# A token mixer without GpSimd: wide head norms, inverse roots by Newton steps on DVE, a sink column, and two projections left in float32

## The chip, the core and the metric

One core of a Trainium2 chip runs the whole program: matrix products on PE (TensorE), elementwise work on DVE (VectorE), ACT (ScalarE) and POOL (GpSimd), loads issued from SP's queue. The metric is the device time of one execution in microseconds. Three executions of the kernel before gave 1207.95, 1210.28 and 1211.51 us; the median, 1210.28 us, is the time before.

## The reference

Two layers of an encoder over 256 tokens of width 1024. A layer is a half-step SwiGLU feed-forward block (FFN, inner width 2816), a token mixer, a second FFN and a gated input embedding. The mixer is what the change is about:

```python
u = rms_norm(h, norm_mix[i])
q, k, v, c, g = jnp.split(u @ w_in[i], splits, axis=-1)      # 512, 128, 128, 1024, 2048 columns
q = rms_norm(q.reshape(B, S, 8, 64), q_norm[i])              # a norm for each head
k = rms_norm(k.reshape(B, S, 2, 64), k_norm[i])
y_attn = window_attention(q, k, v, sink[i], rel_bias) @ w_attn_out[i]
c = c_val * jax.nn.sigmoid(c_gate)                           # c_val, c_gate: halves of c
c = depthwise_conv(c, conv_w[i], conv_b[i])                  # 31 taps, 512 channels
c = jax.nn.silu(layer_norm(c, conv_ln_g[i], conv_ln_b[i]))
y_conv = c @ w_conv_out[i]
g_attn, g_conv = jnp.split(jax.nn.sigmoid(g), 2, axis=-1)
h = h + (g_attn * y_attn + g_conv * y_conv) @ w_o[i]
```

The attention's softmax has one more logit, the sink, which takes weight and gives no value. All inputs are float32.

## The kernel before

Tokens stand in two tiles of 128; a weight is streamed once. `Weights` holds a list of units (loads of up to 1 MB into one of 4 `raw` buffers) and of specs (pieces of 128x1024). `prep_upto` splits each piece into a high part `w_hi` (ACT, L88) and the remainder `w_lo` (DVE, L89), both float32r, into one of 7 pairs of buffers; `get` hands out the next one and prepares the one 6 ahead. `mm3` (L285) makes each product of 128x128 activations with 128x512 weights as three float32r matmuls: high by high (L289), high by low (L290), low by high (L291). Activations are split the same way (`split`, L324). `chunk` runs the products of one output into an accumulator `acc_tile`, of which there are three, and calls the work that empties the accumulator before it (`pending`).

The order on each engine is fixed when the program is built: the framework's scheduler sorts the instructions by priority and by an estimate of when they are ready, and the queues then run in that order. `with_urgency` raises the priority of what it wraps; the taps of the depthwise convolution have the low priority `background`; `ws.later(n, fn)` puts `fn` in front of the n-th weight piece that follows.

The mixer (`mix`, L538) goes through its accumulators in this order: `conv_in(0)` (value and gate of channels 0 to 255), `queries`, `conv_in(2)`, `keys_values`, four `gates`, two `attn_out`, two conv outs (`ps_co`), two outputs of `w_o` (`ps_up`). Beside that run:

- the convolution: after `turn_c` (L584) has put a channel group into `cpad`, 31 taps for each of four channel blocks; blocks 1 to 3 on DVE (first tap L562, the rest L566), block 0 on POOL with two instructions a tap (L559, L560);
- the head norms (`head_norms`, L609): 64-column squares on ACT (L617), `Sqrt` on ACT (L626), reciprocal on DVE, a Newton step of four instructions on POOL (`newton`, L351); then 16 (or 4) scaled copies on ACT (L642, L677), transposes to `qT` and `kT` (L653, L686);
- `scores` (L702): products (L706), bias and row maximum (L716, DVE), negation on POOL, exponentials (L724, ACT), the sink's part on POOL and ACT (L730 to L732), reciprocal, scaling (L735); `attend` transposes the weights (L743), `gather` multiplies by the values (L753);
- the layer norm by token and by channel (L809, L826), whose end (L833) feeds the conv outs, and the splits of `o` (L760) and `y` (L837).

The mean-square norm of the stream (`Norm.finish`, L386) also uses ACT's `Sqrt`, DVE's reciprocal and POOL's Newton step.

## Time and profile before

| what | us |
|---|---|
| executions | 1207.95, 1210.28, 1211.51 (median 1210.28) |
| the profiled execution's own time | 1208.0 |
| its span, first to last instruction | 1206.2 |
| PE busy in the span | 1157.4 (96%) |
| DVE, ACT, POOL busy | 742.5, 625.3, 179.4 |
| mean granted TensorE clock | 0.977 of full speed |

A busy PE is not a PE at its pace: matmuls overlap, and in some stretches the granted clock is half (0.50, which is 1.2 GHz against 2.4 GHz). So the mixer is read by stretches: the time between two starts of the same instruction, the waits of PE with what ended them, and the granted clock. Each time in this text counts from the span's start; the mixer of layer 0 lies between 200 and 380 us, that of layer 1 between 795 and 975 us.

### The profile page before, as it was taken

To read this page: it belongs to the slowest core of one execution; us is meant where nothing else is said; L and a number is where in the kernel's file an instruction comes from. 1 tells how busy PE (TensorE), PEld (TensorE's weight loads), DVE (VectorE), ACT (ScalarE), POOL (GpSimd) and SP (SyncE) were. 2 spreads that over 40 slices of the span, in tenths; PEclk is the share of its full clock that TensorE was granted. 3 is DMA by queue.
4 is the path that set the end of the run, shared out by engine and by line. 5 is a ranking of instruction groups with operands and counts; after the bars stand their busy time and mean duration, and the time that the engine had idled before them with its cause. 6 is when DMAs were issued, how large, how long until landed. Compare 5 with 4: busy or idle time off the path is not lost.

```text
span 1206.2 us, 13732 instructions
## 1 busy us (share of the span) xinstructions
PE 1157.4 (96%) x5138; PEld 923.2 (77%) x5138; DVE 742.5 (62%) x952; ACT 625.3 (52%) x965; POOL 179.4 (15%) x239
## 2 busy tenths in 40 slices
PE   8999999979989999999999999999799899999998
PEld 6778888856667888888878888888566688888886
DVE  6555554689756555545665555557996665555544
ACT  7444444645665545444665444446557555444433
POOL 1000000399300000000100000015990010000001
PEclk9999999978999999999999999999789899999999
DMA  8865455633336565455557555655233365654540
GB/s 280 281 209 198 160 189 180 204 106 74 135 105 183 180 191 188 158 191 174 174 175 209 175 184 183 192 175 177 67 105 121 124 183 184 195 180 158 191 140 36
DMA packets 155360, 202.49 MB, mean 168 GB/s; under 512 B 5284, under 2 KB 108788, under 8 KB 155293
## 3 DMA queue, kind: packets, MB, share of 16 engines
q1 hardware_dynamic: 154204, 200.57, 52.5%
q10 hardware_dynamic: 1088, 1.05, 0.3%
q8 instruction: 40, 0.66, 0.2%
q14 instruction: 28, 0.22, 0.1%
HBM read 200.53 MB, written 1.06 MB: 167 GB/s over the span
## 4 chain that ended last, share of the span: by engine, by line
PE 82%; DVE 6%; POOL 5%; ACT 4%; DMA 2%; issue 1%; SPq 0%; DVEq 0%; ACTq 0%
PE ps_gu L291 13%; PE ps_gu L290 12%; PE ps_gu L289 12%; PE ps_up L291 8%; PE ps_up L289 8%; PE ps_up L290 8%; DVE y L566 3%; POOL part L559 2%; DMA raw<-in_w_ffn_in_dram 2%; PE ps_h L497 2%; PE ps_g L289 1%; PE ps_g L290 1%; POOL y L560 1%; PE ps_g L291 1%; PE ps_o L753 1%
## 5 line engine op out<-in xcount | busy, mean ns | idle before, releaser
L89 DVE TENSOR_TENSOR w_lo<-raw,w_hi 128x1024 fp32r<-128x1024 f32 x376 | 461.4, 1230 | 371.8 <-ACT w_hi L88 371.0
L88 ACT CAST w_hi<-raw 128x1024 fp32r<-128x1024 f32 x376 | 393.6, 1050 | 409.6 <-PE ps_gu L291 192.9
L290 PE MATMUL ps_up<-w_lo,hh 128*128 128x512 f32 x352 | 139.4, 396 | 0.0
L291 PE MATMUL ps_up<-w_hi,hl 128*128 128x512 f32 x352 | 139.4, 396 | 0.0
L289 PE MATMUL ps_up<-w_hi,hh 128*128 128x512 f32 x352 | 139.3, 396 | 0.0
L566 DVE SCALAR_TENSOR_TENSOR y<-cpad,cw,y 128x256 f32<-128x256 f32 x180 | 106.4, 632 | 1.0
L388 POOL TENSOR_TENSOR ms_x<-ss 128x2 f32<-128x2 f32 x8 | 1.7, 217 | 580.8 <-ACT sqj L376 580.8
L291 PEld LDWEIGHTS ps_up<-w_hi,hl 128*128 128x128 f32 x352 | 66.0, 188 | 16.1
L290 PEld LDWEIGHTS ps_up<-w_lo,hh 128*128 128x128 f32 x352 | 66.0, 188 | 15.8
L289 PEld LDWEIGHTS ps_up<-w_hi,hh 128*128 128x128 f32 x352 | 66.0, 188 | 15.7
L559 POOL TENSOR_SCALAR part<-cpad,cw 128x256 f32<-128x256 f32 x60 | 73.3, 1228 | 0.0
L291 PE MATMUL ps_gu<-w_hi,xn0l 128*128 128x512 f32 x176 | 69.1, 395 | 1.2 <-DVE xn0l L327 1.2
L290 PE MATMUL ps_gu<-w_lo,x0h 128*128 128x512 f32 x176 | 70.2, 399 | 0.0
L291 PE MATMUL ps_gu<-w_hi,x0l 128*128 128x512 f32 x176 | 69.7, 396 | 0.0
L290 PE MATMUL ps_gu<-w_lo,xn0h 128*128 128x512 f32 x176 | 69.4, 395 | 0.0
L289 PE MATMUL ps_gu<-w_hi,x0h 128*128 128x512 f32 x176 | 69.4, 394 | 0.0
L290 PE MATMUL ps_gu<-w_lo,xf1h 128*128 128x512 f32 x176 | 69.3, 395 | 0.0
L290 PE MATMUL ps_gu<-w_lo,xf0h 128*128 128x512 f32 x176 | 69.3, 395 | 0.0
L289 PE MATMUL ps_gu<-w_hi,xn0h 128*128 128x512 f32 x176 | 69.0, 393 | 0.0
L291 PE MATMUL ps_gu<-w_hi,xf0l 128*128 128x512 f32 x176 | 69.0, 395 | 0.0
L291 PE MATMUL ps_gu<-w_hi,xf1l 128*128 128x512 f32 x176 | 69.0, 395 | 0.0
L289 PE MATMUL ps_gu<-w_hi,xf1h 128*128 128x512 f32 x176 | 68.9, 393 | 0.0
(234 smaller groups left out, 2078.9 us busy)
## 6 DMA issues: line engine op xcount, KB each, us to landing
raw<-in_w_ffn_in_dram SPq DMA_DIRECT2D x172, 512.0 KB
raw<-in_w_ffn_out_dram SPq DMA_DIRECT2D x40, 1024.0 KB
raw<-in_w_in_dram SPq DMA_DIRECT2D x22, 1024.0 KB
raw<-in_w_in_dram SPq DMA_DIRECT2D x16, 512.0 KB
raw<-in_w_o_dram SPq DMA_DIRECT2D x8, 1024.0 KB
raw<-in_w_pe_gate_dram SPq DMA_DIRECT2D x8, 1024.0 KB
raw<-in_w_ffn_out_dram SPq DMA_DIRECT2D x8, 512.0 KB
raw<-in_w_attn_out_dram SPq DMA_DIRECT2D x8, 512.0 KB
```

The source lines that it names most:

```text
L88: nc.scalar.copy(out=hv[:, :, d0 : d0 + w], in_=src),
L89: nc.vector.tensor_tensor(out=lv[:, :, d0 : d0 + w], in0=src, in1=hv[:, :, d0 : d0 + w].bitcast(F32), op=ALU.subtract,),
L289: nc.tensor.matmul(ps, xh, wh[:, k, :], start=first, stop=False)
L290: nc.tensor.matmul(ps, xh, wl[:, k, :], start=False, stop=False)
L291: nc.tensor.matmul(ps, xl, wh[:, k, :], start=False, stop=last)
L388: nc.gpsimd.tensor_tensor(out=m, in0=self.ss[:, :, 0], in1=self.ss[:, :, 1], op=ALU.add)
L497: nc.tensor.transpose(ps[:, f, tok(t)], hh[:, t, f * P : (f + 1) * P], ident)
L559: nc.gpsimd.tensor_scalar(out=part, in0=src, scalar1=w, scalar2=None, op0=ALU.mult)
L560: nc.gpsimd.tensor_tensor(out=y[:, i, :], in0=part, in1=y[:, i, :], op=ALU.add)
L566: nc.vector.scalar_tensor_tensor(out=y[:, i, :], in0=src, scalar=w, in1=y[:, i, :], op0=ALU.mult, op1=ALU.add)
L753: nc.tensor.matmul(o_ps[qb][v * HD : (v + 1) * HD, :], vt[:, b, v * HD : (v + 1) * HD], pT[:, b, :], start=b == 0, stop=b == 1,)
```

## The change

- **No convolution and no norms on POOL.** The taps of all four channel blocks are DVE's; the first tap of each block, with the bias, is an ACT instruction. POOL keeps eight 128x4 copies of the sink and the fills of `cpad`.
- **Inverse roots on DVE** (`rsqrt` in place of `newton`): a first guess by integer arithmetic and three Newton steps, 11 small instructions one after the other, for the head norms, the stream's norms and the layer norm. ACT's `Sqrt` goes, and with it 10 of 29 table loads.
- **Wide head norms.** One ACT square over all heads, one DVE reduction, `rsqrt`, and four DVE products with `r` broadcast over a head's 64 columns. They are urgent.
- **The order of products**: `conv_in(0)`, `conv_in(2)`, `queries`, `keys_values`.
- **`w_attn_out` and `w_conv_out` aren't split.** Their loads are used as float32 from the `raw` buffer (`raw_spec`), and so are `o` and `y`; `mm3` makes one float32 matmul of such a product in place of three float32r ones. The buffers stay taken until those products are done (`limit`).
- **The sink is a column**: the score tile has 257 columns, signs are turned so that no negation is needed, and the exponential's row sum holds the sink.
- `LOOK` 7 (6), `RAW_BUFS` 5 (4), `W_BUFS` 8 (7), and a smaller scratch for DMA.

The core of the diff:

```diff
@@ Weights
+    def raw_spec(self, unit, k0, k, n):
+        self.specs.append((k, n, [(unit, k0, 0, 0, n)], True))
+    def limit(self):
+        held = [p[0] for s in self.specs[self.next_get : self.next_prep] if s[3] for p in s[2]]
+        return min(held) + RAW_BUFS - 1 if held else len(self.units) - 1
+            if as_is:
+                ((u, k0, s0, _, w),) = pieces
+                self.ready[self.next_prep] = (self.raw[u][:, k0 : k0 + k, s0 : s0 + w],)
@@ mix_specs
             for i in range(0, KC, 2):
-                ws.spec(2, N, [(u, i, 0, 0, N)])
+                ws.raw_spec(u, i, 2, N)
         for c in range(2):
-            block(a["w_conv_out"][l], 0, KC, c * N)
+            u = ws.unit(KC, N, [(whole, rows_of(a["w_conv_out"][l], 0, KC, c * N, N))])
+            for i in range(0, KC, 2):
+                ws.raw_spec(u, i, 2, N)
@@ mm3
+        if len(w) == 1:
+            nc.tensor.matmul(ps, x[:, kx, tok(t)], w[0][:, k, :], start=first, stop=last)
+            return
@@ newton -> rsqrt
+        ri = r.bitcast(I32)
+        nc.vector.tensor_scalar(out=ri, in0=v.bitcast(I32), scalar1=1, scalar2=None, op0=ALU.logical_shift_right)
+        nc.vector.tensor_scalar(out=ri, in0=ri, scalar1=-1, scalar2=0x5F3759DF, op0=ALU.mult, op1=ALU.add)
+        for _ in range(3):
+            nc.vector.tensor_tensor(out=t, in0=r, in1=r, op=ALU.mult)
+            nc.vector.scalar_tensor_tensor(out=t, in0=t, scalar=-0.5, in1=v, op0=ALU.mult, op1=ALU.mult)
+            nc.vector.scalar_tensor_tensor(out=r, in0=t, scalar=1.5, in1=r, op0=ALU.add, op1=ALU.mult)
@@ tap
-                if i == 0:
...
-                    part = tmp.tile([P, T], F32, name="part")
-                    nc.gpsimd.tensor_scalar(out=part, in0=src, scalar1=w, scalar2=None, op0=ALU.mult)
-                    nc.gpsimd.tensor_tensor(out=y[:, i, :], in0=part, in1=y[:, i, :], op=ALU.add)
...
+                if t == 0:
+                    nc.scalar.activation(
+                        out=y[:, i, :], in_=src, func=AF.Identity, scale=w, bias=pcol("conv_b", l, i)
                     )
@@ mix
             conv_in(0)
+            conv_in(2)
...
             queries()
-            conv_in(2)
@@ head_norms
+                nc.scalar.activation(
+                    out=flat.rearrange("p (t n) -> p t n", t=NT), in_=ps[:, :, : heads * HD], func=AF.Square,
+                    scale=HD ** -0.5,
+                )
+                nc.vector.tensor_reduce(
+                    out=ms, in_=flat.rearrange("p (m d) -> p m d", d=HD), op=ALU.add, axis=AX.X
+                )
...
+                rsqrt(r, ms, n)
+                for t in range(NT):
+                    for v in range(2):
+                        hs = slice(v * heads // 2, (v + 1) * heads // 2)
+                        nc.vector.tensor_tensor(
+                            out=out[:, t, :, v, :],
+                            in0=ps[:, t, hs.start * HD : hs.stop * HD].rearrange("p (c d) -> p c d", d=HD),
...
@@ queries
-                    rq = head_norms(acc, NH)
...
+                    with_urgency(lambda: head_norms(qn, acc, NH))
                     ws.later(4, turn_q)
@@ gather
-                    split([p[:, :, tok(qb)] for p in o], ov[:, :, ::-1])
+                    nc.scalar.copy(out=o[:, :, tok(qb)], in_=ov[:, :, ::-1])
@@ ln_by_channel
-                    split([p[:, i : i + 2, :] for p in yp], y[:, i : i + 2, :])
```

What the scheduler makes of it stands in the built order. The first place is the norm of the queries in layer 0. Before, its Newton step is in POOL's queue, among POOL's taps (`part` and `y` are the two instructions of a tap, `nwt` and `rh` the step's tiles, 128x16 for the queries, 128x4 for the keys):

```order
L354 TENSOR_TENSOR nwt<-rh 128x16
L560 TENSOR_TENSOR y<-part,y 128x256
L559 TENSOR_SCALAR part<-cpad,cw 128x256
L355 TENSOR_TENSOR nwt<-nwt,ms 128x16
L623 TENSOR_SCALAR ms<-ms,eps_x 128x2
L559 TENSOR_SCALAR part<-cpad,cw 128x256
L560 TENSOR_TENSOR y<-part,y 128x256
L623 TENSOR_SCALAR ms<-ms,eps_x 128x2
L356 TENSOR_SCALAR nwt<-nwt 128x16
```

Now it is in DVE's queue. It begins so:

```order
L581 SCALAR_TENSOR_TENSOR y<-cpad,cw,y 128x256 x6
L636 TENSOR_REDUCE ms<-qn 128x16
L581 SCALAR_TENSOR_TENSOR y<-cpad,cw,y 128x256 x2
L105 TENSOR_TENSOR w_lo<-raw,w_hi 128x1024
L639 TENSOR_TENSOR ms<-ms,eps_x 128x16
L581 SCALAR_TENSOR_TENSOR y<-cpad,cw,y 128x256 x4
L105 TENSOR_TENSOR w_lo<-raw,w_hi 128x1024
L376 TENSOR_SCALAR rh<-ms 128x16
L581 SCALAR_TENSOR_TENSOR y<-cpad,cw,y 128x256 x2
L636 TENSOR_REDUCE ms<-kn 128x4
```

and ends so, with the normalized queries `qn` and keys `kn`:

```order
L379 TENSOR_TENSOR nwt<-rh 128x4
L581 SCALAR_TENSOR_TENSOR y<-cpad,cw,y 128x256 x2
L647 TENSOR_TENSOR qn<-ps_q,rh 128x4x64 x4
L581 SCALAR_TENSOR_TENSOR y<-cpad,cw,y 128x256 x2
L380 SCALAR_TENSOR_TENSOR nwt<-nwt,ms 128x4
L581 SCALAR_TENSOR_TENSOR y<-cpad,cw,y 128x256 x4
L381 SCALAR_TENSOR_TENSOR rh<-nwt,rh 128x4
L581 SCALAR_TENSOR_TENSOR y<-cpad,cw,y 128x256 x4
L647 TENSOR_TENSOR kn<-ps_kv,rh 128x64 x4
L581 SCALAR_TENSOR_TENSOR y<-cpad,cw,y 128x256 x16
```

From the reduction of the queries to the end of `qn` DVE's queue now holds 50 taps, 7 weight remainders `w_lo`, 22 small instructions and the reduction for the keys; from there to the end of `kn`, 10 taps and 2 small ones. The numbers are the same in layer 1.

The second place is PE at the end of the first gates. Before:

```order
L291 MATMUL ps_g<-w_hi,xm0l 128x512
L653 MATMUL ps_qt<-ident,qn 128x128 x8
L588 MATMUL ps_ct<-ident,hh 128x128 x4
L686 MATMUL ps_kt<-ident,kn 128x128 x2
L706 MATMUL ps_s<-kT,qT 128x256 x4
L289 MATMUL ps_g<-w_hi,xm0h 128x512
```

and now:

```order
L312 MATMUL ps_g<-w_hi,xm0l 128x512
L672 MATMUL ps_qt<-ident,qn 128x128 x8
L697 MATMUL ps_kt<-ident,kn 128x128 x2
L718 MATMUL ps_s<-kT,qT 128x256 x4
L310 MATMUL ps_g<-w_hi,xm0h 128x512
```

The transposes of the second conv group (`ps_ct`) have moved ahead; the transposes of queries and keys and the first scores still stand between the first gates and the second.

The third place is PE at the two projections. They were 96 float32r matmuls in a row of the form `ps_ao<-w_hi,o_h`, with transposes of the layer norm (`ps_yt`, `ps_yc`) between them. Now:

```order
L306 MATMUL ps_ao<-raw,o 128x512
L758 MATMUL ps_o<-pTs,vt 64x512 x2
L306 MATMUL ps_ao<-raw,o 128x512
L814 MATMUL ps_yt<-ident,y 128x128 x4
L834 MATMUL ps_yc<-ident,yn 128x128
L306 MATMUL ps_ao<-raw,o 128x512 x13
L834 MATMUL ps_yc<-ident,yn 128x128 x7
L306 MATMUL ps_ao<-raw,o 128x512
L306 MATMUL ps_co<-raw,y 128x512 x12
L358 MATMUL ps_x<-ident,g 128x128 x4
L306 MATMUL ps_co<-raw,y 128x512 x4
L358 MATMUL ps_x<-ident,g 128x128 x4
```

There are 32 such products in a layer, and the last transposes of the layer norm (`ps_yc`) stand one product ahead of the conv outs.

## Rows read from the trace of the kernel before

**Rows 1.** The page's first part: busy time of PE, DVE and POOL, share of the span, instructions.

```profile
PE 1157.4 (96%) x5138; PEld 923.2 (77%) x5138; DVE 742.5 (62%) x952; ACT 625.3 (52%) x965; POOL 179.4 (15%) x239
```

**Rows 2.** Busy time of each engine in stretches (from:to, length; PE, PE's weight loads, DVE, ACT, POOL, each with its instructions; then granted TensorE clock, DMA share, GB/s): first one of the FFN, then three of layer 0's mixer and five of layer 1's.

```profile
376.00:600.00 224.00, 224.00 (x1015) 182.61 (x1014) 127.20 (x140) 111.74 (x144) 6.26 (x14) 1.00 0.57 183
...
251.74:263.31 11.57, 3.61 (x15) 2.04 (x15) 10.77 (x16) 9.30 (x29) 11.57 (x14) 0.72 0.32 71
...
284.11:290.95 6.84, 6.84 (x19) 5.19 (x20) 6.84 (x12) 6.84 (x17) 6.76 (x7) 0.50 0.69 149
...
345.13:359.88 14.75, 13.61 (x52) 10.52 (x53) 9.69 (x14) 5.15 (x6) 0.00 (x0) 0.88 0.45 142
...
847.08:858.66 11.58, 4.20 (x15) 2.50 (x15) 10.78 (x16) 9.30 (x29) 11.58 (x14) 0.66 0.33 71
858.66:867.80 9.14, 9.14 (x21) 6.31 (x21) 9.14 (x21) 1.25 (x1) 8.76 (x11) 0.50 0.15 27
...
878.15:884.84 6.69, 4.14 (x17) 2.92 (x17) 6.69 (x11) 5.92 (x17) 6.61 (x8) 0.74 0.72 158
884.84:920.80 35.96, 35.96 (x145) 24.59 (x146) 32.40 (x65) 23.97 (x47) 21.49 (x23) 0.95 0.43 141
...
941.39:956.80 15.41, 14.27 (x52) 11.11 (x53) 9.70 (x14) 5.16 (x6) 0.00 (x0) 0.84 0.43 137
```

**Rows 3.** PE's instructions in order of time, layer 0, from the last product of the queries to the first scores (start, length, engine, line; in brackets how long PE stood idle before it, and on whom it waited).

```profile
228.06 0.39 PE L291 MATMUL ps_q<-w_hi,xm0l 128*128 128x512 f32 x1
...
234.91 0.28 PE L289 MATMUL ps_kv<-w_hi,xm0h 128*128 128x256 f32 x1
...
251.35 0.39 PE L291 MATMUL ps_g<-w_hi,xm0l 128*128 128x512 f32 x1
253.80 0.74 PE L653 MATMUL ps_qt<-ident,qn 128*128 128x128 f32 x2 [2.07 <-ACT qn L642]
...
261.86 0.88 PE L686 MATMUL ps_kt<-ident,kn 128*128 128x128 f32 x2 [1.18 <-ACT kn L677]
263.31 1.22 PE L706 MATMUL ps_s<-kT,qT 64*128 64x256 f32 x2 [0.56 <-ACT kT L687]
```

**Rows 4.** The chain of waits between 228 and 264 us: two of its pieces on POOL.

```profile
246.18 1.04 POOL nwt L355
...
251.55 1.04 POOL rh L357
```

**Rows 5.** Who PE waited for, layer 0 from 250 to 365 us (us in total, times, longest), and two lines of the same view of layer 1 that differ.

```profile
PE ps_co L289 <- ACT y_h L326: 4.0, 1, 4.0
...
PE ps_pt L743 <- ACT s L735: 2.2, 1, 2.2
PE ps_yc L831 <- DVE rs L820: 1.7, 1, 1.7
...
PE ps_x L337 <- DVE g L868: 1.1, 1, 1.1
PE ps_up L291 <- DVE ym_l L327: 0.7, 1, 0.7
...
PE ps_pt L743 <- ACT s L735: 1.3, 1, 1.3
PE ps_g L289 <- ACT g L778: 1.2, 1, 1.2
```

**Rows 6.** DVE: the group of all taps in the whole span (busy us, mean ns), then rows in order of time: while POOL is at work (237 to 240 us), and when its last tap is done (from 310.4 us on).

```profile
L566 DVE SCALAR_TENSOR_TENSOR y<-cpad,cw,y 128x256 f32<-128x256 f32 x180 | 106.4, 632 | 1.0
...
237.34 1.21 DVE L89 TENSOR_TENSOR w_lo<-raw,w_hi 128x1024 fp32r<-128x1024 f32 x1
238.48 0.47 DVE L566 SCALAR_TENSOR_TENSOR y<-cpad,cw,y 128x256 f32<-128x256 f32 x1
238.88 0.47 DVE L580 SCALAR_TENSOR_TENSOR hh<-ps_c,r_x,sg 128x256 f32<-128x256 f32 x1
239.27 0.23 DVE L627 RECIPROCAL rh<-rh 128x16 f32<-128x16 f32 x1
239.43 0.41 DVE L566 SCALAR_TENSOR_TENSOR y<-cpad,cw,y 128x256 f32<-128x256 f32 x1
...
310.40 2.06 DVE L566 SCALAR_TENSOR_TENSOR y<-cpad,cw,y 128x256 f32<-128x256 f32 x5
312.38 0.17 DVE L733 RECIPROCAL den<-den 128x4 f32<-128x4 f32 x1
312.46 1.25 DVE L566 SCALAR_TENSOR_TENSOR y<-cpad,cw,y 128x256 f32<-128x256 f32 x3
313.63 0.68 DVE L327 TENSOR_TENSOR o_l<-ps_o,o_h 128x512 fp32r<-128x512 f32 x1
```

**Rows 7.** PE in order of time, 293 to 299 us: float32r matmuls of the gates, the first and the last of twelve, and the float32 products by the values (two in the program, four in the trace).

```profile
293.71 0.39 PE L289 MATMUL ps_g<-w_hi,xm0h 128*128 128x512 f32 x1
...
296.20 0.39 PE L291 MATMUL ps_g<-w_hi,xm0l 128*128 128x512 f32 x1
296.52 1.93 PE L753 MATMUL ps_o<-pTs,vt 128*64 128x512 f32 x4
...
297.00 1.02 PE L753 MATMUL ps_o<-pTs,vt 128*64 128x512 f32 x2
...
297.43 1.02 PE L753 MATMUL ps_o<-pTs,vt 128*64 128x512 f32 x2
```

**Rows 8.** The group of ACT's copies of a 128x1024 accumulator in the mixer of layer 0 (busy us, mean ns, idle before).

```profile
L745 ACT COPY pTs<-ps_pt 128x1024 f32<-128x1024 f32 x4 | 4.1, 1016 | 3.1 <-PE ps_pt L743 3.1
```

More of the change, by code (lines that the diff above doesn't have):

```diff
@@ L40 @@
 ATTN = 5
-W_BUFS = 7
+W_BUFS = 8
 DOWN_TAIL = 3
@@ L61, in spec @@
     def spec(self, k, n, pieces):
-        self.specs.append((k, n, pieces))
+        self.specs.append((k, n, pieces, False))
+    def raw_spec(self, unit, k0, k, n):
[3 more added lines that the diff above has]
+        return min(held) + RAW_BUFS - 1 if held else len(self.units) - 1
     def load_upto(self, u):
-        while self.next_load <= min(u, len(self.units) - 1):
+        while self.next_load <= min(u, self.limit(), len(self.units) - 1):
             k, n, sources = self.units[self.next_load]
@@ L460, in late_tables @@
         tb = hp.tile([NH, NREL], F32, name="tb")
-        nc.vector.tensor_copy(tb, ps[:NH, :NREL])
+        nc.vector.tensor_scalar(out=tb, in0=ps[:NH, :NREL], scalar1=-1.0, scalar2=None, op0=ALU.mult)
+        nc.vector.tensor_scalar(out=late["sink"], in0=late["sink"], scalar1=-1.0, scalar2=None, op0=ALU.mult)
         late["tb"] = tb
@@ L632, in mix @@
-            qn = mp.tile([P, 2, GROUP, 2, HD], F32, name="qn", tag="sqq")
+                flat = out.rearrange("p t c v d -> p (t c v d)")
+                nc.scalar.activation(
[4 more added lines that the diff above has]
+                    out=ms, in_=flat.rearrange("p (m d) -> p m d", d=HD), op=ALU.add, axis=AX.X
+                )
@@ L633, in mix @@
+            qn = mp.tile([P, NT, GROUP, 2, HD], F32, name="qn", tag="sqq")
             qT = mp.tile([P, GROUP, T], F32, name="qT", tag="qT")
@@ L638, in evac @@
                 def evac():
-                    rq = head_norms(acc, NH)
-                    for t in range(2):
-                        for h in range(NH):
-                            nc.scalar.activation(
-                                out=qn[:, t, h % GROUP, h // GROUP, :], in_=acc[:, t, h * HD : (h + 1) * HD],
-                                func=AF.Copy, scale=rq[:, t * NH + h : t * NH + h + 1],
-                            )
+                    with_urgency(lambda: head_norms(qn, acc, NH))
                     ws.later(4, turn_q)
@@ L670, in evac @@
                 def evac():
+                    with_urgency(lambda: head_norms(kn, acc, 2))
                     for t in range(2):
                         nc.scalar.activation(out=vt[:, t, :], in_=acc[:, t, P : 2 * P], func=AF.Copy, scale=st.rt(t))
-                    rk = head_norms(acc, 2)
-                    for t in range(2):
-                        for h in range(2):
-                            s = slice(h * HD, (h + 1) * HD)
-                            nc.scalar.activation(
-                                out=kn[:, t, s], in_=acc[:, t, s], func=AF.Copy,
-                                scale=rk[:, 2 * t + h : 2 * t + h + 1],
-                            )
                     ws.later(3, turn_k)
@@ L692, in mix @@
             keys_values()
[L695 to L698 removed]
+            o = mp.tile([P, GROUP, T], F32, name="o")
             sc = {}
@@ L703, in scores @@
                 ps = acc_tile("ps_s").rearrange("p b (c k) -> p (b c) k", c=2)
-                s = mp.tile([P, GROUP, T], F32, name="s", tag="s", bufs=2)
+                s = mp.tile([P, GROUP, T + 1], F32, name="s", tag="s", bufs=2)
+                h0 = l * NH + v * GROUP
+                nc.gpsimd.tensor_copy(s[:, :, T : T + 1], sink[:, h0 : h0 + GROUP].unsqueeze(2))
                 for c in range(GROUP):
@@ L714, in scores @@
                 for c in range(GROUP):
-                    hd = l * NH + v * GROUP + c
                     nc.vector.tensor_tensor_reduce(
-                        out=s[:, c, :], in0=ps[:, c, :], in1=bias[:, v * GROUP + c, off : off + T],
-                        scale=1.0, scalar=sink[:, hd : hd + 1], op0=ALU.add, op1=ALU.max,
+                        out=s[:, c, :T], in0=ps[:, c, :], in1=bias[:, v * GROUP + c, off : off + T],
+                        scale=1.0, scalar=sink[:, h0 + c : h0 + c + 1], op0=ALU.add, op1=ALU.min,
                         accum_out=nm[:, c : c + 1],
                     )
-                nc.gpsimd.tensor_scalar(out=nm, in0=nm, scalar1=-1.0, scalar2=None, op0=ALU.mult)
                 den = tmp.tile([P, GROUP], F32, name="den")
@@ L801, in attn_out @@
                 pending.append(evac)
-            yp = (
-                mp.tile([P, KC, T], F32R, name="y_h", tag="sqq"),
-                mp.tile([P, KC, T], F32R, name="y_l", tag="qT"),
-            )
             yn = mp.tile([P, NT, N], F32, name="yn", tag="pTs", bufs=2)
@@ L818, in ln_by_token @@
                     rs = tmp.tile([P, 1], F32, name="rs")
-                    nc.scalar.activation(out=rs, in_=mv[:, 1:2], func=AF.Sqrt, bias=eps5)
-                    nc.vector.reciprocal(out=rs, in_=rs)
+                    nc.vector.tensor_scalar(
+                        out=mv[:, 1:2], in0=mv[:, 1:2], scalar1=1e-5, scalar2=None, op0=ALU.add
+                    )
+                    rsqrt(rs, mv[:, 1:2], 1)
                     nc.vector.tensor_scalar(
@@ L876, in mix @@
                 acc = acc_tile("ps_co")
-                chunk(acc, KC, yp, 2 if c else 0, after=lambda t: urgent(t, 1, acc))
+                chunk(acc, KC, y, 2 if c else 0, after=lambda t: urgent(t, 1, acc))
                 if c == 0:
```

87 lines of the change are left out of this document (31 added, 56 removed).

## The prediction

> **What bounds the kernel now.** The page's first part comes first: PE is busy for 96% of the span, DVE, the next, for 62% [rows 1], so a gain has to come from PE's lost time. The table by stretches says where that is: in the FFN, PE is busy for all of 224 us at full clock [rows 2], and nothing there can be won. In the mixer it loses time in two ways. It stands idle: the list of PE's waits [rows 5] and its rows in order of time [rows 3] show some 8 us between the end of the first gates and the first scores, 2.2 us at `ps_pt`, then 1.7, 4.0, 1.1 and 0.7 us from `ps_yc` to `ps_up`. And after each longer gap the granted clock is 0.50 for a while (1.2 instead of 2.4 GHz): for 6.84 us from 284.11 on, for 9.14 us after layer 1's first scores, with means of 0.88 and 0.84 after the gap ahead of `ps_co` [rows 2]. At half clock PE does half its work, so such a stretch costs half its length. The first gap is the largest, and the chain through it lies on POOL, where steps of the Newton iteration (`nwt`, `rh`) take 1.04 us each and queue behind taps [rows 4].
>
> **The change part by part**, in us for one layer; the two layers are alike.
>
> *The head norms.* Both built orders have 970 PE entries ahead of keys and values, so those begin at 234.91 in either [rows 3]. Now the queries' accumulator is finished only then, since the second conv input has moved ahead of it. Cover is what PE does until it needs `qn`: keys, values and first gates. Their last product starts at 251.35 and PE is out of work at 251.74; the second gates can't step in, as their accumulator is the queries' own. The new chain: ACT squares 128x1024 from PSUM, 1.02 by its copy of that size [rows 8], which brings us to 236.1. Then DVE's queue as it stands in the order, piece by piece:
>
> - the reduction of 128x1024. No row shows one; an instruction with as many elements, `w_lo`, takes 1.14 from its start to the next [rows 6]. I take 1.1 (0.9 to 1.4).
> - 50 taps. Five in a row, when POOL does no tap any more, take 2.06, of which the next instruction overlaps a little: 312.38 less 310.40 is 1.98, or 0.396 each [rows 6]. (The mean of all is 0.632, under POOL's load.) 50 x 0.396 = 19.8.
> - 7 `w_lo` at 1.14: 8.0. Their high parts come from ACT; the last is behind the copies of the first gates, about 254, and DVE gets to it at about 255, so no wait is added.
> - 22 small instructions of the inverse roots. Nearest are the reciprocals, 0.08 for 128x4 and 0.16 for 128x16 from start to start [rows 6]. I take 0.10, as a multiplication has less to do than a reciprocal: 2.2 (1.8 to 3.5). Two taps stand between most of them, so no step has to wait for the one before.
> - the keys' reduction and four products of 128x256 from PSUM, as `hh`, 0.39 [rows 6]: 2.0.
>
> That is 33.1, so `qn` is done at 269.2. The keys follow after 10 taps, 2 small instructions and 4 of 128x64: 4.7, at 273.9. From the keys' transposes to the first scores it took 1.45 before [rows 3], so scores begin at 275.3, against 263.31: **+12.0**. With the bounds of the small ones, of the reduction, and `w_lo` at 1.21 [rows 6], +11 to +14.5. This is the heart of it: the old chain was slow on POOL, but the new one is urgent in name only, since its small steps stand in one queue with 60 background taps, and it starts 6.5 later: the queries' last product ended at 228.4 before [rows 3].
>
> A rule of the Trainium skill weighs on the small instructions. The rows give 0.08 to 0.16 for such an instruction. The page "VectorE: DVE Perf Modes", section "The TRN2 errata — SBUF-src ops pay a fixed extra latency per instruction", gives a fixed term of some 150 cycles at 0.96 GHz for each DVE instruction, which speaks against many small ones. As an estimate from that page, 22 of them are 3.7, and the stall 1.5 longer than by the rows; the forecast below would be 3.0 longer.
>
> *Taps off POOL.* DVE gets 30 more taps in a layer, but all at 0.396: 120 are 47.5, where 90 at 0.632 were 57. POOL's part was beside all that. So the rest of the stretch is less crowded: scores, exponentials and scalings are ahead of PE by 3 to 10 when I follow the queues from 275 on, and the wait at `ps_pt` goes with the half clock behind it: 2.2 + 6.84 / 2 = **-5.6** (layer 1: 1.3 + 1.2 + about 3.0 = -5.5). The low clock after the first scores stays: 9.14 at half clock [rows 2] is paid before and after. What is late next there is PE itself.
>
> *Projections in float32.* Twelve float32r matmuls take 2.49 from the first start to the last, 0.226 each, or 0.68 for the three of a product. A float32 product of 512 columns is two records, 0.43 apart (297.00, 297.43): 0.86 [rows 7]. 32 products: 32 x 0.18 = **+5.7**. These rows have 64 stationary columns; 128 are not shown.
>
> *What the missing splits give.* Two splits of `o`, two of `y` and eight weight pieces leave DVE and ACT. At `ps_co` PE waited 4.0 for `y_h`; now the ACT instruction before it is enough, and one 0.86 product covers it. At `ps_x` merges end earlier under slower products. With `ps_yc` and `ps_up` that is 1.7 + 4.0 + 1.1 + 0.7 = **-7.5**, and the clock behind it 0.12 x 14.75 = **-1.8** (layer 1: 0.16 x 15.41 = -2.5). New: in layer 0 the first `ps_yc` waits for the copy of `o`, which stands in ACT's queue behind copies of the last gates, two table loads and a sigmoid: about **+1.6**; in both layers small waits, **+0.5**.
>
> *At nothing.* ACT's first taps (4 at 0.5) and wide squares: ACT is idle for a third of that stretch. Ten table loads: ACT isn't last there. The stream's norms on DVE: PE has a whole accumulator to fill before they are read; without that cover, 11 small steps, 2 us a norm. POOL's sink copies: POOL is idle. Loads: four raw buffers are held by the projections, so the loads of `w_o` pass one by one through the fifth, and the FFN's first wait for the products; by the queue they land 20 us ahead of need, and if not, each would cost PE some 5 us.
>
> **Sum.** Layer 0: 12.0 - 5.6 + 5.7 - 7.5 - 1.8 + 2.1 = +4.9. Layer 1: 12.0 - 5.5 + 5.7 - 7.5 - 2.5 + 0.5 = +2.7. Together +7.6. The profiled execution took 1208.0, so it would take 1215.6; the median of the runs shown is 2.3 above the profiled one, so the median would be 1217.9. I take 1217.
>
> **The rivals.**
>
> *Float32 runs at the pace of float32r (faster).* If a record of a float32 matmul with 128 stationary columns came every 0.226 as float32r's do, a product were 0.45 and the projections would give 32 x 0.23 = 7.4 a layer in place of costing 5.7: 26 less in all, 1191. It decides at 0.74 for a product; below that the kernel is faster than before. Against it: the score products with half the rows and the value products keep the slow pace [rows 7]. The Trainium skill, "FP8 and Floating Point Precision", section "TensorE Precision Notes", has true float32 as four passes through the array, and no row here has that shape. Chance 0.07.
>
> *A shorter queue and a cleaner second half (no change, or a little faster).* The small steps cost 0.08, the reduction 0.9, nothing new waits, and scores and transposes no longer alternate on PE, which may save another 1 to 2 in switches. A layer is then 11 - 5.6 + 5.7 - 7.5 - 2.2 - 1.5 = -0.1: 1210, between 1204 and 1213. For it: each term is within its rows. Chance 0.25.
>
> *More is lost behind the longer gap (slower).* PE is now almost without work for 24 us. If the low clock lasts longer after that, and a chain in the second half comes late (the sigmoid of the gates now stands before the last exponentials in ACT's queue), a layer pays 14.5 + 4 + 3 more small waits: 1228, up to 1233. For it: clocks of 0.66 and 0.72 in the first gap [rows 2]. Chance 0.18.
>
> *It doesn't do what it says*: taps leave POOL by construction, so nothing is left here.
>
> **How the numbers follow.** The forecast, 1213 to 1223, has 0.50; the rivals 0.07, 0.25, 0.18. The range takes in the second and third rival: 1203 to 1230. What a measurement of this kernel can tell from no change is 0.3%, or 3.6 us: slower means above 1214. The forecast puts 0.45 there and 0.05 under it, the third rival 0.18; of the second, 0.12 are within and 0.13 faster; the first is faster. Slower 0.63, same 0.17, faster 0.20.
>
> **What would show it.** PE's first transposes of `qn` near 269 and scores near 275 in layer 0, with the chain of waits on DVE taps in place of POOL; taps at about 0.40 each; no gap at `ps_pt`; float32 products 0.86 apart; no gap of 4 us ahead of `ps_co`. The prediction fails if `qn` is ready before 260, if products are faster than 0.74, or if the gaps behind the scores stay.

## The result

| | us |
|---|---|
| before, 19 executions | median 1209.89 (1207.95 to 1211.51) |
| after, 19 executions | median 1212.15 (1210.57 to 1213.34) |
| ratio | 1.0020, 95% interval 1.0013 to 1.0027 |
| profiled execution of after | 1212.65, span 1210.9, mean clock 0.977 |

The changed kernel is slower by 2.3 us (1.6 to 3.3 by the interval). That is surely more than nothing and less than the 0.3% that counts as slower here. The forecast was 1217, seven above the time before.

The first line of the page, against [rows 1]: POOL is all but empty, ACT has 42 us less, and DVE, which took over the taps and the inverse roots, is no busier than before.

```profile
PE 1155.3 (95%) x5074; PEld 906.0 (75%) x5074; DVE 736.9 (61%) x1187; ACT 583.2 (48%) x803; POOL 5.7 (0%) x21
```

PE in order of time ahead of the first scores of layer 0, against [rows 3] (start, length, what; in brackets the idle time before):

```profile
252.50 0.39 PE L312 MATMUL ps_g<-w_hi,xm0l 128*128 128x512 f32 x1
269.25 2.16 PE L672 MATMUL ps_qt<-ident,qn 128*128 128x128 f32 x8 [16.37 <-issue]
274.32 0.66 PE L697 MATMUL ps_kt<-ident,kn 128*128 128x128 f32 x2 [2.91 <-DVE kn L647]
275.55 2.07 PE L718 MATMUL ps_s<-kT,qT 64*128 64x256 f32 x4 [0.56 <-ACT kT L698]
```

One gap of 16.4 us, with one of 2.9 behind it, stands where four small ones stood. DVE in the middle of it: two taps between any two steps of the inverse roots, as the built order had it.

```profile
257.08 0.16 DVE L379 TENSOR_TENSOR nwt<-rh 128x4 f32<-128x4 f32 x1
257.15 0.88 DVE L581 SCALAR_TENSOR_TENSOR y<-cpad,cw,y 128x256 f32<-128x256 f32 x2
257.94 0.17 DVE L379 TENSOR_TENSOR nwt<-rh 128x16 f32<-128x16 f32 x1
258.03 0.88 DVE L581 SCALAR_TENSOR_TENSOR y<-cpad,cw,y 128x256 f32<-128x256 f32 x2
258.82 0.16 DVE L380 SCALAR_TENSOR_TENSOR nwt<-nwt,ms 128x4 f32<-128x4 f32 x1
```

A small step costs 0.07 to 0.09 from its start to the next, a pair of taps 0.79. Who PE waited for in layer 0 (250 to 370 us), against [rows 5]: `ps_co`, `ps_pt` and `ps_up` are gone, `ps_x` has stayed, and the new wait at `ps_yc` is for the copy of `o`.

```profile
PE ps_qt L672 <- issue: 16.4, 1, 16.4
PE ps_kt L697 <- DVE kn L647: 2.9, 1, 2.9
PE ps_yc L834 <- ACT o L765: 1.3, 1, 1.3
PE ps_x L358 <- DVE g L870: 1.2, 1, 1.2
PE ps_s L718 <- ACT kT L698: 0.6, 1, 0.6
```

The products in float32 (first row: 26 records, the last starts one step ahead of 348.19), and of before the first and the last of 14 float32r matmuls of the same projection:

```profile
337.03 11.32 PE L306 MATMUL ps_ao<-raw,o 128*128 128x512 f32 x26
348.19 0.93 PE L834 MATMUL ps_yc<-ident,yn 128*128 128x128 f32 x7
```

```profile
337.72 0.39 PE L290 MATMUL ps_ao<-w_lo,o_h 128*128 128x512 f32 x1
...
340.75 0.40 PE L291 MATMUL ps_ao<-w_hi,o_l 128*128 128x512 f32 x1
```

So a record takes (348.19 - 337.03) / 26 = 0.429 and a product 0.86; before, 3.03 / 13 = 0.233 a matmul and 0.70 a product.

Where the time went is read from the mixer cut at five places that both kernels have: the starts of the first `ps_c` and of the first scores, the ends of the last `ps_pt`, `ps_co` and `ps_up` (columns as in [rows 2]). Before, layer 0 and then layer 1:

```profile
196.60:263.31 66.71, 58.74 (x286) 48.17 (x284) 47.31 (x62) 42.08 (x107) 34.34 (x44) 0.95 0.54 169
263.31:320.91 57.60, 55.45 (x212) 39.57 (x213) 57.26 (x115) 32.73 (x72) 46.53 (x51) 0.88 0.30 85
320.91:360.05 39.14, 32.28 (x130) 23.29 (x131) 20.22 (x30) 23.99 (x29) 0.00 (x0) 0.96 0.36 124
360.05:385.80 25.75, 25.04 (x118) 19.91 (x118) 17.09 (x21) 12.77 (x19) 0.00 (x0) 1.00 0.56 172
791.95:858.66 66.71, 59.33 (x285) 48.63 (x284) 47.31 (x62) 42.09 (x107) 34.34 (x44) 0.94 0.55 169
858.66:917.17 58.51, 55.96 (x212) 39.57 (x213) 57.30 (x115) 32.72 (x72) 46.58 (x51) 0.86 0.31 89
917.17:956.97 39.80, 32.95 (x130) 23.86 (x131) 20.22 (x30) 24.00 (x29) 0.00 (x0) 0.91 0.35 115
956.97:982.71 25.74, 25.04 (x118) 19.91 (x118) 17.09 (x21) 12.77 (x19) 0.00 (x0) 1.00 0.57 172
```

After:

```profile
197.29:275.55 78.26, 58.41 (x286) 48.31 (x284) 64.24 (x148) 34.60 (x47) 1.06 (x4) 0.88 0.52 149
275.55:326.27 50.72, 50.72 (x206) 36.61 (x207) 37.37 (x98) 33.98 (x69) 1.50 (x2) 0.92 0.22 71
326.27:365.70 39.43, 36.94 (x106) 17.61 (x106) 17.84 (x44) 15.01 (x18) 0.00 (x0) 1.00 0.46 149
365.70:390.33 24.63, 24.63 (x119) 20.05 (x117) 15.27 (x19) 11.82 (x18) 0.00 (x0) 1.00 0.52 161
795.64:873.90 78.26, 58.37 (x285) 48.32 (x284) 64.24 (x148) 34.62 (x47) 1.06 (x4) 0.87 0.51 149
873.90:922.44 48.54, 48.54 (x199) 35.47 (x200) 36.47 (x96) 33.77 (x69) 1.18 (x2) 0.93 0.20 65
922.44:962.71 40.27, 38.84 (x112) 18.41 (x113) 18.59 (x45) 15.23 (x18) 0.00 (x0) 1.00 0.49 157
962.71:987.37 24.66, 24.66 (x118) 20.05 (x117) 15.28 (x19) 11.82 (x18) 0.00 (x0) 1.00 0.52 156
```

Up to the scores a layer loses 78.26 - 66.71 = 11.55, in both layers. From there to the end of `ps_up` it gets back 122.49 - 114.78 = 7.7 in layer 0 and 124.05 - 113.47 = 10.6 in layer 1. Layer 0 is 3.8 longer and layer 1 1.0; the start of the program is 0.7 later, and layer 0's embedding, which no longer waits 0.81 ahead of `ps_pp`, 0.8 shorter: 4.7 for this pair of executions, twice the distance of the medians. What the pair has to do with the medians is the last of the experiments.

### The profile page after: what moved, and what is told of

Same layout as the page of the kernel before. It is cut to its first block, busy times and chain, and to the rows that moved or that the text cites. A ratio compares the mean times of both kernels' runs of the same rounds, so it can differ in the third digit from the quotient of the medians.

```text
span 1210.9 us, 13444 instructions
## 1 busy us (share of the span) xinstructions
PE 1155.3 (95%) x5074; PEld 906.0 (75%) x5074; DVE 736.9 (61%) x1187; ACT 583.2 (48%) x803; POOL 5.7 (0%) x21
## 4 chain that ended last, share of the span: by engine, by line
PE 90%; DVE 7%; issue 1%; ACT 1%; DMA 1%; ACTq 0%; DVEq 0%
PE ps_gu L310 13%; PE ps_gu L312 13%; PE ps_gu L311 13%; PE ps_up L310 8%; PE ps_up L311 8%; PE ps_up L312 8%; DVE y L581 4%; PE ps_co L306 2%; PE ps_g L310 2%; PE ps_ao L306 2%; PE ps_g L311 2%; PE ps_g L312 2%; PE ps_h L521 2%; PE ps_s L718 2%; PE ps_x L358 1%; PE ps_pe L312 1%
## 5 line engine op out<-in xcount | busy, mean ns | idle before, releaser
L105 DVE TENSOR_TENSOR w_lo<-raw,w_hi 128x1024 fp32r<-128x1024 f32 x360 | 439.6, 1224 | 356.9 <-ACT w_hi L104 356.3
L104 ACT CAST w_hi<-raw 128x1024 fp32r<-128x1024 f32 x360 | 376.6, 1051 | 412.9 <-PE ps_gu L312 202.9
L581 DVE SCALAR_TENSOR_TENSOR y<-cpad,cw,y 128x256 f32<-128x256 f32 x240 | 101.7, 478 | 0.0
L310 PE MATMUL ps_gu<-w_hi,xf0h 128*128 128x512 f32 x176 | 69.1, 393 | 0.0
L513 DVE SCALAR_TENSOR_TENSOR hh<-ps_gu,r_x,sg 128x256 f32<-128x256 f32 x88 | 42.1, 479 | 3.5 <-ACT sg L512 3.5
```

The source lines that it names most:

```text
L104: nc.scalar.copy(out=hv[:, :, d0 : d0 + w], in_=src),
L105: nc.vector.tensor_tensor(out=lv[:, :, d0 : d0 + w], in0=src, in1=hv[:, :, d0 : d0 + w].bitcast(F32), op=ALU.subtract,),
L310: nc.tensor.matmul(ps, xh, wh[:, k, :], start=first, stop=False)
L513: nc.vector.scalar_tensor_tensor(out=hh[:, t, :], in0=acc[:, t, 256:], scalar=x.rt(t), in1=sg, op0=ALU.mult, op1=ALU.mult)
L581: nc.vector.scalar_tensor_tensor(out=y[:, i, :], in0=src, scalar=w, in1=y[:, i, :], op0=ALU.mult, op1=ALU.add)
```

## The experiments

**The theory** at the start: the prediction's terms are right in kind; the gap is the queue of taps and its late start, the unsplit projections and the emptier POOL pay it back. **The rivals**: the gap would be there without the taps; the waits behind the scores came from POOL and not from the splits; the taps' slower pace was not POOL's doing. Ratios are against the kernel before, in the same set of runs; the changed kernel's is 1.0020.

### e1: the norms ahead of the taps

```diff
-                        for t in range(TAPS):
+                        for t in range(FREE_TAPS):            # 2
...
+                    with tc.issue_after(kn_done.ins):         # last product of the keys' norm
+                        for t in range(FREE_TAPS, TAPS): ...  # the other taps, on DVE behind it
```

> The changed kernel, with all taps but the first two of each block put behind the last product of the keys' norm on DVE (order only, no wait). Theory A (the gap is the queue: 50 taps at 0.396 and 7 w_lo at 1.14 stand between the steps of the inverse root): from the square at 236.1 the queue to qn is then reduction 1.1, three w_lo 3.4, two taps 0.8, some 20 small ones 2.0, the products 1.6: qn near 246, inside the first gates, which end at 252.9. No gap ahead of the transposes of qn, none of the 27.3 us at half clock: idle 19.9 and half clock 5.5 a layer gone, about 1162 (1160 to 1172). The taps end late, near 310 by the work that DVE has, against a need near 312. Rival B (the late start and the dependent steps' own latency make the gap, not the taps): qn not before 260, 1195 to 1205. Rival C (the taps become the bound: pushed back behind 248, with w_lo and the scores' reductions between, they end near 330 where PE needs y at 312): PE waits some 15 to 20 us a layer ahead of ps_yt, 1200 to 1212.

Measured: 1195.05 us, ratio 0.9875 (0.9859 to 0.9892), between the ranges of A and C. The first part of A holds within some 1 us: `qn` was done at 247.2, and the stretch up to the scores fell from 78.3 to 59.2 in both layers, though a wait of 2.45 ahead of the scores is left, which A did not have. But 19.1 a layer was won there and only 8.5 at the end. Most of the rest went into a wait at the norm of `y`: from the last `ps_pt` to the last `ps_co` a layer takes 9.4 to 9.8 longer (PE, then DVE):

```profile
256.88 1.65 PE L727 MATMUL ps_s<-kT,qT 64*128 64x256 f32 x3 [2.45 <-ACT kT L707]
...
329.10 1.04 PE L823 MATMUL ps_yt<-ident,y 128*128 128x128 f32 x8
337.60 0.45 PE L843 MATMUL ps_yc<-ident,yn 128*128 128x128 f32 x1 [7.46 <-DVE yn L833]
```

```profile
309.60 5.23 DVE L582 SCALAR_TENSOR_TENSOR y<-cpad,cw,y 128x256 f32<-128x256 f32 x13
318.85 1.23 DVE L106 TENSOR_TENSOR w_lo<-raw,w_hi 128x1024 fp32r<-128x1024 f32 x1 [4.03 <-ACT w_hi L105]
...
324.70 0.47 DVE L582 SCALAR_TENSOR_TENSOR y<-cpad,cw,y 128x256 f32<-128x256 f32 x1
```

DVE reached a piece of `w_o` at 314.8, stood 4.0 us waiting for its high part, which ACT, busy with the gates and two table loads until then, began at 317.8; the last seven taps stood behind it. A further piece, ahead of the norm of `y`, waited for a load that passes through the fifth raw buffer. Neither A nor C had this: the taps ended at 325 instead of 310, and without those pieces the last seven (0.395 each) would have ended at 317.6.

### e2: the old product order

```diff
-            conv_in(0)
-            conv_in(2)
-            queries()
+            conv_in(0)
+            queries()
+            conv_in(2)
```

> The changed kernel with the products in the order of the kernel before (conv_in 0, queries, conv_in 2, keys and values); norms, taps and projections as changed. Theory A (the queue and its start both count): the queries end near 229.4 again, the square is done at 230.4, and by the built order 10 w_lo (11.4), 2 hh (0.8), 20 taps (7.9), 14 small ones (1.4), two reductions (1.4) and the products (1.6) stand up to qn: qn near 255, scores near 262, so 13 to 14 us a layer less than the changed kernel: 1184 (1180 to 1192). Rival B (what counts is the queue alone, and it fills again: the chain ends where the background lets it): scores at 270 or later, 1203 to 1212.

Measured: 1195.02, ratio 0.9876 (0.9861 to 0.9891): 3 above A's range and 17 us below the changed kernel, so the order of the products alone cost it some 8.5 a layer. `qn` came at 254.5, as expected, and the scores 4.9 later than expected:

```profile
253.88 0.44 PE L671 MATMUL ps_qt<-ident,qn 128*128 128x128 f32 x2 [1.22 <-DVE qn L646]
...
265.65 0.66 PE L697 MATMUL ps_kt<-ident,kn 128*128 128x128 f32 x2 [9.22 <-DVE kn L646]
```

With the queries out of the way, the keys are last: four taps, 1.6 us, stand between the last steps of their norm. Both causes of theory A count, and the queue moves to the next chain.

### e3: the splits of the projections back

```diff
-                ws.raw_spec(u, i, 2, N)
+                ws.spec(2, N, [(u, i, 0, 0, N)])              # attn_out and conv_out
-                    nc.scalar.copy(out=o[:, :, tok(qb)], in_=ov[:, :, ::-1])
+                    split([p[:, :, tok(qb)] for p in o], ov[:, :, ::-1])   # and y likewise
```

> The changed kernel with attn_out and conv_out as three float32r products again, so o and y split and eight weight pieces a layer back on ACT and DVE. Theory A (the sum of the prediction: the waits at ps_co, ps_x and ps_up come from the splits): products get 32 x 0.16 = 5.1 a layer shorter, waits of 4 to 7.5 and some half clock return: within 3 of the changed kernel, 1209 to 1218, with PE waiting some 4 us ahead of ps_co for y_h. Rival B (those waits came from POOL's slow steps and taps, not from the splits): they stay away, and 5 a layer are won: 1200 to 1204.

Measured: 1220.8, ratio 1.0090 (1.0075 to 1.0105), 8.5 above the changed kernel. B falls, and so does A's "within 3". The waits that came back, layer 0 (250 to 380 us):

```profile
PE ps_co L310 <- ACT y_h L347: 4.9, 1, 4.9
...
PE ps_x L358 <- DVE g L878: 1.1, 1, 1.1
PE ps_up L312 <- DVE ym_l L348: 0.7, 1, 0.7
```

`ps_co` and `ps_up` are the splits' own; `ps_x` waits 1.1 with them and 1.2 without, so it never was. The mean clock from the last `ps_pt` to the last `ps_co` is 0.92 and 0.88 (1.00 in the changed kernel): 0.08 x 41.5 and 0.12 x 43.5, some 8.5 us of lost clock in both layers, part of it while PE waits. Leaving the projections unsplit was worth some 4 us a layer, more than the sum of the prediction gave it (1.5 and 3.8).

### e4: the first block's taps on GpSimd again

```diff
+                if i == 0:
+                    nc.gpsimd.tensor_scalar(out=part, in0=src, scalar1=w, ...)
+                    nc.gpsimd.tensor_tensor(out=y[:, i, :], in0=part, in1=y[:, i, :], op=ALU.add)
```

> The changed kernel with the 31 taps of the first block back on GpSimd, as before. Theory A (POOL's taps slow DVE's: 0.632 against 0.396): 40 taps instead of 50 stand ahead of qn, at 0.632: 25.3 against 19.8, so the scores begin 5.5 later, near 281, and the wait at ps_pt with half clock behind it returns in part: 8 to 10 a layer, 1228 to 1234. Rival B (0.632 was not POOL's doing): 40 taps at 0.40, the scores 4 earlier, 1202 to 1206.

Measured: 1226.24, ratio 1.0135 (1.0120 to 1.0150), 2 under A's range. B falls; A holds for the gap, which is 5.2 to 6.5 longer although ten taps fewer stand in it. The group of taps on DVE, here and in the changed kernel (busy us, mean ns):

```profile
L590 DVE SCALAR_TENSOR_TENSOR y<-cpad,cw,y 128x256 f32<-128x256 f32 x180 | 106.9, 646 | 0.2
```

```profile
L581 DVE SCALAR_TENSOR_TENSOR y<-cpad,cw,y 128x256 f32<-128x256 f32 x240 | 101.7, 478 | 0.0
```

Sixty taps more, in less time. A tap has two inputs in SBUF. The Trainium skill, "SBUF — State Buffer", section "SBUF: two separate sides", says that such a DVE instruction and a GpSimd instruction that reads SBUF take a shared pair of ports from each other for a whole instruction; 646 against 478 ns agrees with that.

A's second part does not hold: the wait at `ps_pt` did not return. From the first scores to the last `ps_pt` PE is busy all the time in layer 0, and the 1.4 that it waits in layer 1 is for something else (ahead of `ps_g`); the two stretches are about as long as the changed kernel's (50.72 and 48.54):

```profile
282.07:330.54 48.47, 48.47 (x196) 35.42 (x197) 34.39 (x81) 33.10 (x69) 18.91 (x21) 0.91 0.19 66
...
884.92:935.22 50.30, 48.93 (x195) 35.54 (x196) 35.95 (x82) 33.92 (x69) 18.99 (x23) 0.90 0.18 63
```

### e6: one piece less looked ahead

```diff
-LOOK = 7
+LOOK = 6
-W_BUFS = 8
+W_BUFS = 7
```

> The changed kernel with one weight piece less looked ahead and kept (LOOK 6, W_BUFS 7, as before; five raw buffers stay). Theory A (the 0.8 us that layer 0's embedding no longer waits ahead of ps_pp comes from the longer look-ahead): that wait comes back, the start of the first FFN changes by some tenths, 1212.5 to 1213.5. Rival B (it comes from the shorter norm of the stream, which has nothing to do with the pieces): no wait there, the time within 0.5 of the changed kernel's. Rival C (pieces are late for the mixer too): 1215 or more.

Measured: 1210.84, ratio 1.0005 (0.9996 to 1.0013). The wait ahead of `ps_pp` did not return, so A and C fall. B has the mechanism, but not its "within 0.5": by the ratios the run is 1.8 us faster than the changed kernel, with intervals that just touch. The longer look-ahead gave nothing here.

### e7, e8, e9: what stands behind the gap

`e7_norms_old_order` is e1 and e2 together. `e8_wo_behind` is e1 with this, and `e9_combo` has all three:

```diff
+            if wo and self.behind is None:                    # no piece of w_o before the norm of y is traced
+                return
...
+                with tc.issue_after(self.behind):             # last instruction of the norm of y
                     nc.vector.tensor_tensor(out=lv, in0=src, in1=hv, op=ALU.subtract)
```

> The changed kernel with the norms ahead of the taps and the products in the order of the kernel before, both together. With the taps behind the norm alone, qn was done at 247.2 and the scores stood at 256.9 behind a wait of 2.45 for the keys; the last seven taps then stood behind pieces of w_o that waited for their load, and PE waited 1.7 and 7.5 us around ps_yt and ps_yc. Theory A (DVE's taps, with those pieces ahead of them, now set the end): qn near 240 and kn near 246, no wait ahead of the scores, but y only 3 to 5 earlier and the wait at ps_yc stays at 5 or more: 1186 to 1193. Rival B (with the gap the rest goes too): 1170 to 1178.

> The changed kernel with the norms ahead of the taps, and the pieces of w_o put behind the norm of y on DVE (order only) instead of ahead of the last taps. Theory A (the 9.2 us that PE then waited around ps_yt and ps_yc are those pieces, which waited for their raw buffer): taps end near 316 instead of 325, no wait at ps_yc, no half clock behind it, 11 us a layer less than with the norms alone: 1172 (1168 to 1179). Rival B (DVE's own work is the bound; the pieces stood in its idle time): taps end at 321 or later, 1187 to 1195. Rival C (the pieces come too late for the products with w_o): a new wait ahead of ps_up of 4 to 10, 1180 to 1195.

> All three moves together: norms ahead of the taps, products in the order of the kernel before, pieces of w_o behind the norm of y. Theory A (each takes away its own wait): the 2.45 ahead of the scores goes as well, 2 to 3 us a layer under the kernel without the old product order: 1167 (1162 to 1174). Rival B (once PE doesn't wait for the norms, the end of the taps is the bound, and an earlier start doesn't move it): equal to that kernel within 2.

Measured: e7 1192.6 (0.9838 to 0.9865), e8 1187.77 (0.9796 to 0.9827), e9 1195.4 (0.9858 to 0.9885). e7 goes by A in its time and in the wait at `ps_yc` (6.5); but the scores were no earlier (255.9), with a wait of 2.7 ahead of them that A did not have. In e8 the taps ended at 314.5, as A has it, yet the time is 9 above A's range: PE still waited 2.4 for `yn` in layer 0, and 3.9 for it and 2.7 for `y` in layer 1. The built order has the transposes of `y` at 326.2, deep in the second half of attn_out. In e9, 8 us slower than e8, both theories fall: PE waited 2.7 for `yn` and 4.6 for `y`. ACT shows where the 4.6 come from:

```profile
334.86 1.99 ACT L108 CAST w_hi<-raw 128x1024 fp32r<-128x1024 f32 x2 [4.42 <-DMA raw<-in_w_o_dram]
336.87 1.28 ACT L852 ACT_TABLE_LOAD   x1
338.17 1.93 ACT L852 ACTIVATE y<-ps_yc,par 128x256 f32<-128x256 f32 x4
```

Only the low parts of `w_o` had been moved; the high parts stand on ACT ahead of the last activation of `y`, and wait for loads that pass one by one through the fifth raw buffer. This is what the prediction had priced at "some 5 us" if the loads came late. In the changed kernel PE's list shows no such wait.

### e10: the stream's norm on GpSimd again

```diff
-            rsqrt(self.r, m, NT)
+            nc.scalar.activation(out=self.r, in_=m, func=AF.Sqrt)
+            nc.vector.reciprocal(out=self.r, in_=self.r)
+            newton(self.r, m, NT)                             # four instructions on GpSimd
```

> The changed kernel with the stream's norm (the seven inverse roots of the residual stream) on GpSimd, ACT and DVE again, as before. Theory A (the 0.8 us that the embedding of layer 0 no longer waits ahead of ps_pp is the shorter norm): that wait comes back, 0.5 to 2 us more: 1212.5 to 1214. Rival B (it comes from the order of the rest): no wait there, the same time within 0.5. Rival C (the inverse root on DVE costs more than it gives, since it stands in DVE's queue): faster by over 1.

Measured: 1214.01, ratio 1.0038 (1.0026 to 1.0051), 2.1 above the changed kernel in the same set (1211.93). Theory A: the wait ahead of `ps_pp` is back, with layer 0's embedding 0.9 longer.

```profile
608.43 0.50 PE L310 MATMUL ps_pp<-w_hi,pTh 128*128 128x512 f32 x1 [0.81 <-DVE sge L919]
```

The prediction had put this norm down at nothing, for the better or the worse.

### e11: the norm of y at its place on PE

This is `e8_wo_behind` with one edit more:

```diff
+            with tc.issue_after(late["yt"]):                  # last transpose of y
                 attn_out(1)
```

> The kernel with the norms ahead of the taps and the pieces of w_o behind the norm of y, and on PE all of y's transposes ahead of the second half of attn_out (order only). There the taps ended at 314.5, the first half at about 316, but the transposes stood at 325.8, so that PE then waited 2.4 (layer 1: 3.9 and 2.8) for yn and y. Theory A (the place on PE makes that wait): the norm of y is done at about 323 under the second half, which ends at 324 to 325; no wait over 1.5 at ps_yc and none ahead of ps_co, 3 to 7 us a layer less, with the half clock of layer 1: 1177 (1172 to 1181). Rival B (taps end too late for it): PE waits at ps_yt instead, 1185 to 1190.

Measured: 1183.7, ratio 0.9785 (0.9768 to 0.9803): 26 us below the kernel before, the best of all. Rival B falls. What PE still waits for in layer 0:

```profile
PE ps_ao L312 <- ACT o L780: 2.8, 1, 2.8
PE ps_s L733 <- ACT kT L713: 2.4, 1, 2.4
PE ps_x L364 <- DVE g L887: 2.0, 1, 2.0
PE ps_co L312 <- ACT y L852: 0.6, 1, 0.6
```

No wait at `ps_yc` is left. The time is 2.7 above the expected range, which had not counted the wait for `o` (2.8 a layer).

### The two kernels once more

> The kernel before, unchanged, profiled in another execution. The prediction added 2.3 us to its sum, the distance between the median and the one profiled execution. Theory A (that distance is chance of the one execution, and lies in two places: the first wait for weights in the first FFN, and where the half-clock stretches fall): the first FFN's length moves by 0.5 to 1.2 and the stretch from the scores to the last ps_pt by 0.5 to 2, all others by under 0.2; time anywhere from 1208 to 1211.5. Rival B (executions of a kernel are alike, and the distance is fixed): every stretch within 0.2, time within 0.5 of 1208.0.

> The changed kernel, unchanged, profiled in another execution. Theory A: the first FFN's length moves by 0.5 to 1.2, the stretch from the scores to the last ps_pt by up to 2 (in the kernel with LOOK 6 it was 2.5 and 0.4 shorter than in the profiled execution), the gap ahead of the scores by under 0.2. Rival B: every stretch within 0.2, time within 0.5 of 1212.65.

Measured: before 1210.09 in the profiled execution (1208.0 in the first), after 1212.22 (1212.65). Rival B falls for both: stretches move by more than 0.2. After goes by A; before only in part, since its first FFN did not move (187.7 and 187.6) and 0.6 lies behind the last `ps_pt`, where A had under 0.2. Of before, these two stretches of layer 0 are 0.9 and 0.6 longer than in the first execution, with a mean clock of 0.87 and 0.91 instead of 0.88 and 0.96:

```profile
263.66:322.13 58.47, 56.01 (x212) 39.52 (x213) 57.27 (x115) 32.74 (x72) 46.57 (x51) 0.87 0.31 89
322.13:361.89 39.76, 32.90 (x130) 23.87 (x131) 20.21 (x30) 24.00 (x29) 0.00 (x0) 0.91 0.34 114
```

That is 1.5 of the 2.1 between the two executions. In the stretches up to the scores and of `ps_up` no execution of a kernel differs from its other by more than 0.04. Of after, the first FFN was 0.9 longer and the second half 0.7 and 0.5 shorter. This pair differs by 2.1, as the medians do: layer 0 by 1.7, layer 1 by 0.2.

## Why the prediction was off

The sign was right, and so was the mechanism of the gap. The size was not: +7 was forecast, +2.3 came, and the time lies 0.9 under the forecast's 1213 to 1223. By its own steps:

- **Head-norm chain, +12.0.** +11.50 to +11.55 a layer, in both pairs of executions; the transposes of `qn` began at 269.25 against 269.2, the scores at 275.55 against 275.3. That the times agree so closely is in part luck: layer 0 began 0.7 later, and the reduction stood behind six taps and began at 237.46 instead of 236.1, but the queue from there to the end of `qn` took 32.3 instead of 33.1. e1 and e2 show both of its reasons: without the taps in between the stretch is 19.1 shorter, with the old order 8.5 to 8.9. The estimates of a tap (0.396 against some 0.395), of the reduction (1.1 against 1.13) and of small steps (0.10 against 0.07 to 0.09) held. So the estimate of 3.7 from the Trainium skill, "VectorE: DVE Perf Modes", section "The TRN2 errata — SBUF-src ops pay a fixed extra latency per instruction", was too dear for steps with other work between. Where they stand back to back and depend on each other, as the last of the keys' in e1, a step took 0.19.
- **Taps off POOL, -5.6.** The size fits: the wait at `ps_pt` is gone, and the stretch from the scores to the last `ps_pt` is 6.9 and 10.0 shorter. The reason is not borne out: e4 shows POOL's taps as the cause of the slower tap and of a longer gap, but with them back the wait stayed away. What took it away no run shows. The sink column, which takes POOL's steps out of the chain ahead of the scaling, and the new order on DVE were not undone alone.
- **Missing splits, -7.5, and the clock, -1.8 and -2.5.** e3 shows the waits at `ps_co` and `ps_up` as the splits' own; the 1.7 at `ps_yc` came back in layer 1 alone (2.0). The 1.1 at `ps_x` stayed, with another 1.3 at `ps_yc` (forecast 1.6). The clock gave more. One minus the mean clock, times the stretch, from the scores to the last `ps_co` (it counts PE's waits in): before 8.5 and 11.8, in the other execution 11.2 and 10.0; after 4.1 and 3.4, in the other 3.5 and 3.4. So 4.4 and 8.4, or 7.7 and 6.6, where the prediction, with 3.4 behind `ps_pt`, had 5.2 and 5.5. Both reckon a stretch at half clock as half lost. It is a little less: in the kernel before, float32r matmuls of `ps_co` came every 0.427 at a clock of 0.51 (345.84 to 348.40), against 0.233.
- **Projections in float32, +5.7.** Mis-sized: a product is 0.86, as forecast, but the three matmuls that it replaces took 0.70, not 0.68, since the pace came from the gates' matmuls ([rows 7], 0.226) and not from the projections' own (0.233). 32 x 0.16 = 5.1. The rival in which float32 runs at float32r's pace falls.
- **At nothing.** The stream's norm is worth 2.1 in all (e10), of which the profile shows 0.8; the longer look-ahead is worth nothing or less (e6).

From the scores to the end of `ps_up` the terms made -7.1 for layer 0 and -9.3 for layer 1; measured were -7.7 and -10.6, and -9.9 and -11.3 in the other pair. **The steps that failed** are these. The sum's second half was 1.7 a layer too dear, by the projections (0.6) and the clock (1.4 by the measure above), with small waits up and down. And in the last step **the 2.3 between the profiled execution of before and its median was added to the new time as if it went with the program.** It does not: with 19 executions the distance is 1.9, the changed kernel's median lies 0.5 under its own profiled execution, and the second profile of before has 1.5 of its 2.1 between the scores and the last `ps_co`, where the granted clock is lower. That the changed kernel has little left to lose there fits its 3.4 to 4.1 of lost clock, but is argued.

Of the 4.9 between 1217 and 1212.15, 3.0 are the sum's (1215.6 against 1212.65 in the profiled execution), 1.4 are what the forecast put on top of it, and 0.5 is the distance of the new median from its profile. The sizes of the small terms are not sharper than this: the two pairs of profiled executions differ by 4.7 and 2.1, the medians by 2.3.

The second rival, a shorter queue and a cleaner second half (1210, between 1204 and 1213), has the measured time in its range: its small steps (0.08) are what the rows show, its reduction (0.9) is not, and whether fewer switches on PE save anything no run tells. The third rival falls: behind the first scores the clock was 0.50 for 8.2 and 7.2 us, against 7.1 and 9.1 before ([rows 2] has the 9.14). Its price did not follow from its terms either: 2.5, 4 and 3 a layer above the forecast are 1236, not 1228. And of the eight Newton steps in the view of [rows 4] three take 1.04 to 1.09, the others 0.17 to 0.37, so "1.04 us each" read too much into two rows.

In the last stretch, up to the end of `ps_up`, PE's busy time fell by 0.4 a layer, and not in e3. No work became cheaper there: before and in e3 twelve transposes of `g` (`ps_x`) stand in it, in the changed kernel eight, since four start at 365.54, just ahead of the cut. That the median of before exceeds its first profile by half clock rests on one further execution.

## What to carry to other kernels

A change that gives an engine free room can be eaten by the order in which the room is used: moving the second conv input ahead cost 8.5 a layer and leaving background work between the steps of an urgent chain as much, while unsplit projections gave 4 and the emptied POOL 7. Such prices do not add: with both moves undone (e7) some 10 a layer came back, not 17. Price each part by undoing it alone, and after each wait removed look for the next queue it uncovers. Make the sum against the profiled execution and ask, before the distance to the median is added, in which stretch that distance lies: if the change rebuilds that stretch, it doesn't carry over.
